# Tile order inside a weight chunk, a bias table written in eight pieces, S5 prefetches tied to late weight loads, and an S5 inner product at foreground priority

## The chip, the cores and the metric

The program runs on one core of a Trainium2 chip. The time is that of one execution in device microseconds (us); three executions of the kernel before were timed, and one further execution was profiled. The engines are named as in the profile: PE is TensorE (its weight loads apart as PEld), DVE is VectorE, ACT is ScalarE, POOL is GpSimd, SP is SyncE, which here only issues DMAs.

## The reference, cut to what matters

Two transformer blocks of width 2048 run over 256 positions in float32.

```python
def first_block(x, p, ...):
    z = rms_norm(x, norm_mix_pre) @ w_in
    y_lru = rglru_mixer(u, g_lru, ...)               # gated recurrence
    y_nsa = nsa_mixer(q, kc, vc, ..., rel_bias)      # sparse attention; bias_tab[rel_bucket(dist)]
    h = x + rms_norm(concat(norms(y_lru, y_nsa)) @ w_out)
    h = h + rms_norm(square(relu(rms_norm(h) @ mlp_w1)) @ mlp_w2)
    return h + sigmoid(h @ ple_gate) * (p @ ple_proj)

def second_block(x, ...):
    # layer 0: stick-breaking attention and gated linear attention, then swiglu_ffn(0)
    # layer 1: s5_mixer, then swiglu_ffn(1)

def s5_mixer(h, ...):        # 128 groups of 16 channels, 64 complex states each
    s_re, s_im = scan(lambda, b @ u)
    y = gelu(c_re @ s_re - c_im @ s_im + d * u)
    val, gate = split(y @ w_glu)
    return val * sigmoid(gate)

def swiglu_ffn(h, w_in, w_out):
    gate, up = split(h @ w_in)
    return (silu(gate) * up) @ w_out
```

## The kernel before, in words

**Dense products.** Activations lie transposed: 128 features on the partitions, T=256 positions in a row. A float32 product is made of fp32r products. A weight chunk lands in a `wr` tile (`wload`, SP issues the DMA at L258); ACT casts it to `wh` (L261), DVE subtracts to get the rest `wl` (L262). X is kept as a high and a low half side by side. For each 128 features of the input (index `kk` in a chunk, usually two to a chunk) and each output tile `j` (usually four, one PSUM bank each) PE does `wh` times both halves (512 columns) and `wl` times the high half (256 columns), both at L304 in `group`. "Narrow" groups put two tiles into a bank and need three matmuls of 256 columns. At a group's end `evac` empties each tile: ACT copies one half (L357), DVE adds the other (L361, or L364 and L365 with a factor), and the bank is free for a later group. PSUM tiles have the tags `ps`, `px` and `pm`.

**Order.** A scheduler orders each engine's instructions by priority, which is the place in the program unless `low(n)` moves it back; each engine runs its list in order. `issue_after(i)` puts an instruction behind `i` in the same engine's list without a wait. A DMA whose completion semaphore is still in use by an earlier DMA waits for that one.

**Background work.** `s5_gen` builds the matrices of the S5 mixer (DRAM tensors `TTd`, `TBd`, `BBd`, `CBd`) while the MLP of the first block and ffn(0) of the second run, at a priority lowered by 100 (`bg_low`). For each of its 16 blocks `prod` does eight small matmuls into one bank `kt` (L1720). In the first mixer a list `self.mix` of generators is advanced by two steps after each chunk (`mix_step`): compression of keys and values, the position bias, and the gated recurrence.

**Bias table.** `bias_tables` makes one row of 511 bias values per head with one matmul (`tb`, 16 partitions), and one DMA of POOL (L608) writes a skewed table `tab` of 16 x 128 x 256 values to DRAM, from which the mixer reads back (`m<-tab`).

**S5 stage.** Eight loads bring `TBd` (L1803) and six bring part of `TTd` (L1901: two into `ttq`, four into an `x` tile); then `carry`, `turn`, `inner` and `outer` run over 8 pairs of feature tiles. `wraw` (L1794) loads `BBd`, `TTd` and `CBd` into slots of the weight pool. After `outer`, ACT applies gelu (L1930), and `relay` (L1812) moves finished ranges of k (`cuts`: 0 to 8, 8 to 12, 12 to 16) from `Yg` to `Yt` in eight SBUF-to-SBUF DMAs each, from 16 partitions apiece. `pre` (L1948, L1949) splits the result into halves for the GLU product, a `group` with `pre`.

Of the kernel before, what the change touches and what calls it, by code (L numbers as in the profile page):

```python
# [57 lines left out]
def layout(inp):  # L58
# [28 lines left out]
    o["relb"] = rb  # L87
    dist = np.arange(511) - 255
    b = np.where(dist >= 0, _rel_bucket(dist), 32)
    oh = np.zeros((33, 2, 511), np.float32)  # L90
    oh[b, 0, np.arange(511)] = 1.0
    oh[:, 1] = oh[:, 0, ::-1]
# [44 lines left out]
class K:  # L137
    def __init__(self, tc, I, out, es, dump=None):
        self.tc, self.nc, self.I, self.out = tc, tc.nc, I, out
        self.es = es  # L140
        self.dumpf = dump
        pool = lambda name, bufs, **k: es.enter_context(tc.tile_pool(name=name, bufs=bufs, **k))
        self.cp = pool("const", 1)
        self.xp = pool("xp", 6)
        self.wp = pool("wp", 4)
        self.ep = pool("ep", 5)
        self.mp = pool("mp", 9)
        self.sp = pool("sp", 4)
# [5 lines left out]
        self.mix, self.mix_n, self.summed = [], 1, None  # L154
        self.hold = ()
# [97 lines left out]
    def wload(self, pieces, shape=(P, 2, 512)):  # L253
# [3 lines left out]
        for sl, src in pieces:  # L257
            nc.sync.dma_start(wr[sl], src)  # L258
# [28 lines left out]
    def group(self, Xk, ks, load, ntile=4, pre=None, narrow=None, tag="ps", kc=2):  # L287
# [17 lines left out]
        for c in range(0, n, kc):  # L305
# [4 lines left out]
            for kk in range(kc):  # L310
                i = c + kk
                X = Xk(ks[i])
                for j in range(ntile):
                    if narrow:
                        mm(ps[j], lhs(wh, kk, j), X[:, 0], i == 0 and j % 2 == 0, False)
                        mm(ps[j], lhs(wh, kk, j), X[:, 1], False, False)
                        mm(ps[j], lhs(wl, kk, j), X[:, 0], False, i == n - 1)
                    else:
                        mm(ps[j], lhs(wh, kk, j), X, i == 0, False)
                        mm(ps[j][:, 0:T], lhs(wl, kk, j), X[:, 0], False, i == n - 1)  # L320
# [274 lines left out]
    def bias_tables(self):  # L595

        nc, I = self.nc, self.I
        relb = self.m([33, 16], tag="relb", bufs=1)
        nc.scalar.dma_start(relb, I["relb"])
        oh = self.wp.tile([33, 2, 511], F32, tag="wr", name="oh")  # L600
        nc.scalar.dma_start(oh, I["oh"])
        ps = self.ps()
        nc.tensor.matmul(ps[0:16, 0:511], relb, oh[:, 1], start=True, stop=True)
        tb = self.m([16, 512])
        nc.vector.tensor_copy(tb[:, 0:511], ps[0:16, 0:511])
# [18 lines left out]
    def block1_in(self):  # L624
# [39 lines left out]
        self.mix, self.mix_n = [self.compress_gen(kk, cmp_), self.bias_gen(), self.lru_gen(L)], 2  # L664
# [854 lines left out]
    def s5_gen(self):  # L1519
# [193 lines left out]
        def prod():  # L1713
# [3 lines left out]
            for i in range(2):  # L1717
                for r in range(4):
                    q = 2 * r + i
                    nc.tensor.matmul(kt[r * 32:r * 32 + 32, 0:P], bt[:, i, r * 32:r * 32 + 32],  # L1720
                                     cx[q // 4][:, q % 4].rearrange("p t h -> p (t h)"), start=(i == 0), stop=(i == 1),
                                     skip_group_check=True)
# [74 lines left out]
    def s5(self):  # L1797
# [126 lines left out]
        def outer(kp):  # L1924
# [83 lines left out]
```

## Time and profile before

| | |
|---|---|
| Median of three executions | 3652.32 us (3651.43 to 3671.67) |
| Profiled execution, its own time | 3657.45 us |
| Its span | 3655.6 us |
| Mean granted TensorE clock | 0.981 |
| PE busy | 3501.3 us, 96% |
| PEld busy | 3060.9 us, 84% |
| DVE, ACT, POOL busy | 64%, 50%, 28% |
| DMA | 699.60 MB, mean 191 GB/s |

PE's busy time is a sum of modelled pipelined intervals, so small gaps between matmuls hide in it. The page's slices show where it falls; the waits show what it stood for. Rows of the trace say start, duration, engine, line, operation, and in brackets the idle time before and what ended it.

### The profile page before, as it was taken

To read this page: it belongs to the slowest core of one execution; us is meant where nothing else is said; L and a number is where in the kernel's file an instruction comes from. 1 tells how busy PE (TensorE), PEld (TensorE's weight loads), DVE (VectorE), ACT (ScalarE), POOL (GpSimd) and SP (SyncE) were. 2 spreads that over 40 slices of the span, in tenths; PEclk is the share of its full clock that TensorE was granted. 3 is DMA by queue.
4 is the path that set the end of the run, shared out by engine and by line. 5 is a ranking of instruction groups with operands and counts; after the bars stand their busy time and mean duration, and the time that the engine had idled before them with its cause. 6 is when DMAs were issued, how large, how long until landed. Compare 5 with 4: busy or idle time off the path is not lost. (4 is left out here: it accounts for less than half of the span.)

```text
span 3655.6 us, 59158 instructions
## 1 busy us (share of the span) xinstructions
PE 3501.3 (96%) x22198; PEld 3060.9 (84%) x22198; DVE 2353.4 (64%) x3610; ACT 1833.1 (50%) x2879; POOL 1022.5 (28%) x1498
## 2 busy tenths in 40 slices
PE   8989999999999999999899999999779999999998
PEld 8888888888888898999787888887668888888887
DVE  6686785567656866546765566566755765555566
ACT  4656654644445654346644444344555544444444
POOL 1231242299620112104334555465400200000000
PEclk9999999999999999999999999999989999999999
DMA  8644456667765564565567776677875466665663
GB/s 216 207 130 151 130 172 189 181 210 211 229 202 187 180 198 135 149 194 187 161 207 227 225 228 211 212 225 246 261 219 185 144 192 188 190 187 188 187 187 127
DMA packets 506551, 699.60 MB, mean 191 GB/s; under 512 B 43239, under 2 KB 317671, under 8 KB 506264
## 3 DMA queue, kind: packets, MB, share of 16 engines
q1 hardware_dynamic: 472848, 628.60, 55.8%
q0 software_dynamic: 27120, 63.05, 5.8%
q10 hardware_dynamic: 6296, 4.17, 0.4%
q8 instruction: 174, 2.85, 0.3%
q14 instruction: 113, 0.93, 0.1%
HBM read 654.22 MB, written 37.22 MB: 189 GB/s over the span
## 5 line engine op out<-in xcount | busy, mean ns | idle before, releaser
L304 PE MATMUL ps<-x,wh 128*128 128x512 f32 (+1 forms) x8560 | 2498.4, 355 | 62.1 <-DVE e L361 19.3
L262 DVE TENSOR_TENSOR wl<-wr,wh 128x1024 fp32r<-128x1024 f32 x1126 | 1441.4, 1285 | 1099.6 <-ACT wh L261 1095.3
L304 PE MATMUL ps<-x,wl 128*128 128x256 f32 x6832 | 1922.4, 283 | 0.8 <-DVE wl L262 0.8
L261 ACT ACTIVATE wh<-wr 128x1024 fp32r<-128x1024 f32 x1126 | 1184.0, 1057 | 1245.0 <-PE ps L304 1051.9
L304 PEld LDWEIGHTS ps<-x,wh 128*128 128x128 f32 x8560 | 1510.7, 191 | 319.5 <-issue 30.3
L304 PEld LDWEIGHTS ps<-x,wl 128*128 128x128 f32 x6832 | 1306.1, 191 | 11.1 <-issue 5.6
L304 PE MATMUL px<-x,wh 128*128 128x512 f32 (+1 forms) x1776 | 658.3, 396 | 11.2 <-DVE x L249 6.8
L304 PE MATMUL px<-x,wl 128*128 128x256 f32 x1744 | 491.7, 282 | 0.5 <-DVE wl L262 0.5
L304 PEld LDWEIGHTS px<-x,wh 128*128 128x128 f32 x1776 | 332.6, 189 | 94.4 <-DVE x L249 8.6
L304 PEld LDWEIGHTS px<-x,wl 128*128 128x128 f32 x1744 | 330.5, 190 | 4.8 <-issue 3.2
L527 POOL TENSOR_TENSOR e<-x,r_c 128x256 f32<-128x256 f32 x40 | 39.8, 1001 | 1051.0 <-DVE r_c L448 1042.8
L357 ACT ACTIVATE e<-ps 128x256 f32<-128x256 f32 x324 | 120.5, 377 | 75.2 <-PE ps L304 63.4
L1762 POOL TENSOR_TENSOR m<-m,m 128x128 f32<-128x128 f32 x128 | 70.3, 573 | 302.5 <-PE pm L1720 302.5
L376 POOL TENSOR_TENSOR acc<-acc,sq 128x256 f32<-128x256 f32 x89 | 78.0, 876 | 252.7 <-ACT sq L375 250.0
L245 ACT ACTIVATE x<-e 128x256 fp32r<-128x256 f32 x168 | 68.2, 411 | 90.1 <-DVE e L1500 47.3
L246 DVE TENSOR_TENSOR x<-e,x 128x256 fp32r<-128x256 f32 x168 | 86.0, 521 | 26.4 <-ACT x L245 22.6
L1761 POOL TENSOR_TENSOR m<-m,m 128x128 f32<-128x128 f32 x128 | 82.7, 671 | 0.7
L1779 POOL TENSOR_TENSOR m<-m,m 128x256 f32<-128x256 f32 x64 | 59.6, 932 | 71.7 <-DMA m<-in_s5bT_dram 71.0
L361 DVE TENSOR_TENSOR e<-ps,e 128x256 f32<-128x256 f32 x168 | 69.9, 416 | 6.4 <-ACT e L357 6.4
L1780 POOL TENSOR_TENSOR m<-m,m 128x256 f32<-128x256 f32 x64 | 73.7, 1152 | 0.1
L738 PE MATMUL ps<-wh,x 128*128 128x512 f32 x160 | 64.6, 404 | 0.0
L740 PE MATMUL ps<-wh,x 128*128 128x512 f32 x160 | 63.2, 395 | 0.0
(488 smaller groups left out, 2895.3 us busy)
## 6 DMA issues: line engine op xcount, KB each, us to landing
wr<-in_w_ffn_in_dram SPq DMA_DIRECT2D x704, 256.0 KB, 3.3
wr<-in_mlp_w_dram SPq DMA_DIRECT2D x256, 512.0 KB, 4.2
wr<-in_w_ffn_out_dram SPq DMA_DIRECT2D x176, 512.0 KB, 4.3
wr<-in_w_in_dram SPq DMA_DIRECT2D x152, 512.0 KB, 3.8
wr<-in_w_out_dram SPq DMA_DIRECT2D x64, 512.0 KB, 4.1
wr<-in_w_glu_dram SPq DMA_DIRECT2D x128, 256.0 KB, 3.1
wr<-in_ple_gate_dram SPq DMA_DIRECT2D x32, 512.0 KB, 4.5
wr<-in_w_in_dram SPq DMA_DIRECT2D x32, 256.0 KB, 4.9
```

Source lines behind the costliest of these rows:

```text
L245: a = nc.scalar.activation(dst[:, 0], src, AF.Copy)
L246: b = (eng or nc.vector).tensor_tensor(dst[:, 1], src, dst[:, 0].bitcast(F32), op=ALU.subtract)
L261: nc.scalar.activation(wh, wr, AF.Copy)
L262: nc.vector.tensor_tensor(wl, wr, wh.bitcast(F32), op=ALU.subtract)
L304: mm = lambda o, w, x, a, z: nc.tensor.matmul(o, w, x, start=a, stop=z, skip_group_check=True)
L357: a = S.activation(t, ps[:, T:2 * T], AF.Copy)
L361: self.hold = a, V.tensor_tensor(y, ps[:, 0:T], t, op=ALU.add)
L376: (eng or nc.vector).tensor_tensor(acc, acc, q, op=ALU.add)
L738: nc.tensor.matmul(ps, xh, wh, start=first, stop=False, skip_group_check=True)
L1761: G_.tensor_tensor(cx[:, q], u_(0), l_(0), op=ALU.mult)
L1762: G_.tensor_tensor(t1[:, q], u_(1), l_(1), op=ALU.mult)
L1780: G_.tensor_tensor(t1, v4(gb[0][:, 1]), v4(gb[1][:, 1 - ri]), op=ALU.mult)
```

## The change

It has five parts.

- **Tile order.** In each chunk `group` now runs all matmuls of tile 0, then of tile 1, and so on. Only in groups with `pre` the chunks before the last keep the old order (all tiles of one `kk`, then of the next).
- **Inner product.** The eight matmuls of `prod` get the priority of foreground work.
- **Bias table.** The table `relb` is repeated eight times, so that `tb` fills 128 partitions; eight POOL DMAs, each from another 16 partitions, write 16 of the 128 rows of `tab` each. They stand in a generator, first in `self.mix`, one per step. `oh` is taken from the `m` pool and not from a `wr` slot.
- **S5 prefetches.** The `TBd` loads are tied behind every third of the last 25 weight loads of ffn(0), and the six `TTd` loads behind the last one.
- **Relays.** From `Yg` to `Yt` the first range is issued by POOL alone, the other two by POOL and SP in turn; ACT issues none.

```diff
@@ bias_tables
-        relb = self.m([33, 16], tag="relb", bufs=1)
+        relb, oh = self.m([33, P], tag="relb", bufs=1), self.m([33, 512])
...
-        oh = self.wp.tile([33, 2, 511], F32, tag="wr", name="oh")
...
-        skew = bass.AP(tensor=tb.tensor, offset=tb.offset + 127, ap=[list(tb.ap[0]), [-1, P], [1, T]])
-        nc.gpsimd.dma_start(self.tab, skew)
+        def gen():
+            for r in range(8):
+                rows = tb[r * 16:r * 16 + 16]
+                nc.gpsimd.dma_start(self.tab[:, r * 16:r * 16 + 16], bass.AP(
+                    tensor=rows.tensor, offset=rows.offset + 127 - 16 * r, ap=[list(rows.ap[0]), [-1, 16], [1, T]]))
+                yield 1
+        self.tab_gen = gen()
...
-        self.mix, self.mix_n = [self.compress_gen(kk, cmp_), self.bias_gen(), self.lru_gen(L)], 2
+        self.mix, self.mix_n = [self.tab_gen, self.compress_gen(kk, cmp_), self.bias_gen(), self.lru_gen(L)], 2
@@ group
-            for kk in range(kc):
+            order = [(kk, j) for j in range(ntile) for kk in range(kc)]
+            if pre and c + kc < n:
+                order = [(kk, j) for kk in range(kc) for j in range(ntile)]
+            for kk, j in order:
@@ s5_gen, prod
-            for i in range(2):
-                for r in range(4):
+            with self.low(-self.bg_low):
+                for i in range(2):
+                    for r in range(4):
@@ s5
+        late = self.loads[-25:]
         for kp in range(8):
-            nc.sync.dma_start(TB[kp // 4][:, kp % 4], self.TBd[kp])
+            with self.tc.issue_after(late[3 * kp].ins):
+                nc.sync.dma_start(TB[kp // 4][:, kp % 4], self.TBd[kp])
...
-                nc.sync.dma_start(tl[:, i], tt_src(len(tts)))
+                with self.tc.issue_after(late[-1].ins):
+                    nc.sync.dma_start(tl[:, i], tt_src(len(tts)))
...
-                    relay(Yg, Yt, k0, k1, (nc.gpsimd, nc.scalar) if i < 2 else (nc.gpsimd, nc.scalar, nc.sync))
+                    relay(Yg, Yt, k0, k1, (nc.gpsimd, nc.sync) if i else (nc.gpsimd,))
```

The first place is PE's list at the end of a group in the MLP of the first block, where the last chunk of one group (`px_7806` to `ps_7809`, and `px_7813` to `ps_7816` after) is followed by the first chunk of the next. Before:

```order
L304 MATMUL px_7806<-x_5333,wh_7966 128x512
L304 MATMUL px_7806<-x_5333,wl_7967 128x256
L304 MATMUL px_7807<-x_5333,wh_7966 128x512
L304 MATMUL px_7807<-x_5333,wl_7967 128x256
L304 MATMUL ps_7808<-x_5333,wh_7966 128x512
L304 MATMUL ps_7808<-x_5333,wl_7967 128x256
L304 MATMUL ps_7809<-x_5333,wh_7966 128x512
L304 MATMUL ps_7809<-x_5333,wl_7967 128x256
L304 MATMUL ps_8056<-x_5332,wh_8062 128x512
```

After, in the same place:

```order
L304 MATMUL ps_7815<-x_5340,wh_7973 128x512
L304 MATMUL ps_7815<-x_5340,wl_7974 128x256
L304 MATMUL ps_7815<-x_5340,wh_7973 128x512
L304 MATMUL ps_7815<-x_5340,wl_7974 128x256
L304 MATMUL ps_7816<-x_5340,wh_7973 128x512
L304 MATMUL ps_7816<-x_5340,wl_7974 128x256
L304 MATMUL ps_7816<-x_5340,wh_7973 128x512
L304 MATMUL ps_7816<-x_5340,wl_7974 128x256
L304 MATMUL ps_8063<-x_5339,wh_8069 128x512
```

The last four pairs of the group went round all four tiles before; now they are the two pairs of the third tile and the two of the fourth, and the first two tiles have ended ahead of them.

The second place is PE's list where the eight matmuls of one block's `prod` (into a `pm` bank) stand among those of ffn(0). Before:

```order
L1720 MATMUL pm_21057<-m_20366,m_20345 32x128
L304 MATMUL px_21094<-x_18759,wh_21209 128x512
L1720 MATMUL pm_21057<-m_20366,m_20345 32x128
L304 MATMUL px_21094<-x_18759,wl_21210 128x256
L1720 MATMUL pm_21057<-m_20596,m_20345 32x128
L304 MATMUL ps_21095<-x_18759,wh_21209 128x512
L1720 MATMUL pm_21057<-m_20596,m_20345 32x128
L304 MATMUL ps_21095<-x_18759,wl_21210 128x256
L304 MATMUL ps_21096<-x_18759,wh_21209 128x512
L1720 MATMUL pm_21057<-m_20366,m_20345 32x128
```

After, for the same block:

```order
L1732 MATMUL pm_21064<-m_20373,m_20352 32x128 x2
L1732 MATMUL pm_21064<-m_20603,m_20352 32x128
L304 MATMUL px_21100<-x_18765,wh_21106 128x512
L1732 MATMUL pm_21064<-m_20603,m_20352 32x128
L304 MATMUL px_21100<-x_18765,wl_21107 128x256
L1732 MATMUL pm_21064<-m_20373,m_20352 32x128
L304 MATMUL px_21100<-x_18765,wh_21106 128x512
L1732 MATMUL pm_21064<-m_20373,m_20352 32x128
L304 MATMUL px_21100<-x_18765,wl_21107 128x256
L1732 MATMUL pm_21064<-m_20603,m_20352 32x128
```

The block before was eight runs of one matmul; after it is a run of three and five of one. Seven of the 16 blocks had eight runs and have six now; eight had five runs (four matmuls and then one at a time), and have five still.

The third place is SP's list where `CBd` is loaded for the last pairs of the S5 stage. Before, the last two loads stand together:

```order
L1794 DMA wl_27905<-CBd 128x1024
L1794 DMA wr_27915<-CBd 128x1024
L1794 DMA wl_27933<-CBd 128x1024
L1794 DMA wr_27943<-CBd 128x1024
L258 DMA wr_27980<-in_w_glu_dram 128x2x256 x2
```

After, four relays of the second range stand between them:

```order
L1806 DMA wl_27912<-CBd 128x1024
L1806 DMA wr_27922<-CBd 128x1024
L1806 DMA wl_27940<-CBd 128x1024
L1826 DMA x_27579<-x_27578 128x1x128 x4
L1806 DMA wr_27950<-CBd 128x1024
L258 DMA wr_27987<-in_w_glu_dram 128x2x256 x2
```

The relays came to SP from ACT's list, and the last load moved behind them.

## Rows read from the trace of the kernel before

**Rows 1.** The page: busy time of the engines, and granted TensorE clock by slices.

```profile
PE 3501.3 (96%) x22198; PEld 3060.9 (84%) x22198; DVE 2353.4 (64%) x3610; ACT 1833.1 (50%) x2879; POOL 1022.5 (28%) x1498
...
PEclk9999999999999999999999999999989999999999
```

**Rows 2.** PE's waits: line waited for, us in total, times, longest us.

```profile
PE ps L304 <- DVE e L361: 19.3, 14, 2.9
PE ps L304 <- ACT wh L261: 14.1, 4, 7.5
...
PE ps L304 <- DVE e L364: 5.5, 5, 3.4
...
PE pm L870 <- ACT wh L261: 2.5, 1, 2.5
```

**Rows 3.** Busy time by stretches; PE first, then the granted clock, DMA share, GB/s.

```profile
100.00:200.00 100.00, 89.07 (x594) 80.64 (x592) 68.96 (x116) 62.18 (x108) 33.93 (x51) 0.92 0.64 192
...
2600.00:2700.00 100.00, 62.77 (x901) 48.57 (x901) 68.35 (x99) 48.85 (x80) 32.73 (x51) 0.78 0.87 261
```

**Rows 4.** PE's timeline at a group end in the MLP of the first block.

```profile
716.54 0.39 PE L304 MATMUL ps<-x,wh 128*128 128x512 f32 x1
...
716.89 0.39 PE L304 MATMUL ps<-x,wh 128*128 128x512 f32 x1
719.13 0.47 PE L304 MATMUL ps<-x,wh 128*128 128x512 f32 x1 [1.85 <-DVE e L361]
```

**Rows 5.** DVE's timeline of the same stretch.

```profile
715.83 1.64 DVE L262 TENSOR_TENSOR wl<-wr,wh 128x1024 fp32r<-128x1024 f32 x1
717.39 1.26 DVE L246 TENSOR_TENSOR x<-e,x 128x256 fp32r<-128x256 f32 x2
718.57 0.41 DVE L361 TENSOR_TENSOR e<-ps,e 128x256 f32<-128x256 f32 x1
```

**Rows 6.** PE's timeline at one block's inner product in ffn(0).

```profile
2118.22 0.43 PE L1720 MATMUL pm<-m,m 128*32 128x128 f32 x8
2118.57 0.50 PE L304 MATMUL ps<-x,wh 128*128 128x512 f32 x1
2119.00 0.41 PE L1720 MATMUL pm<-m,m 128*32 128x128 f32 x2
2119.34 0.39 PE L304 MATMUL ps<-x,wl 128*128 128x256 f32 x1
```

**Rows 7.** Stretch of a block of eight runs, first run to last.

```profile
1992.92:1998.39 5.47, 5.47 (x25) 2.51 (x24) 1.22 (x1) 0.70 (x1) 1.25 (x4) 1.00 0.63 191
```

**Rows 8.** DMA issues, 58 to 92 us: queues; KB each, median us to landing.

```profile
q0 software_dynamic: 528, 2.10, 57.9%
...
tab<-m POOLq DMA_DIRECT2D x1, 2048.0 KB, 25.5
wr<-in_w_in_dram SPq DMA_DIRECT2D x8, 256.0 KB, 14.4
```

**Rows 9.** PE's timeline near 84 us; busy time of 84 to 89 us.

```profile
84.77 0.80 PE L304 MATMUL ps<-x,wh 128*128 128x256 f32 x2 [5.73 <-ACT wh L261]
...
84.00:89.00 5.00, 3.77 (x16) 3.48 (x17) 1.54 (x2) 1.78 (x2) 0.00 (x0) 0.50 1.02 307
```

**Rows 10.** DMA queues and issues from 2604 to 2614 us, relays of the S5 stage.

```profile
q0 software_dynamic: 192, 0.52, 26.3%
...
x<-x POOLq DMA_DIRECT2D x4, 128.0 KB, 5.0
```

**Rows 11.** DMA issues from 2480 to 2520 us, the W2 product of ffn(0).

```profile
wr<-in_w_ffn_out_dram SPq DMA_DIRECT2D x12, 512.0 KB, 5.7
x<-TBd SPq DMA_DIRECT2D x8, 512.0 KB, 7.9
```

**Rows 12.** PE's timeline, stalls at 2010 and 2507 us in ffn(0).

```profile
2010.17 0.50 PE L304 MATMUL ps<-x,wh 128*128 128x512 f32 x1 [1.98 <-DVE x L361]
...
2506.77 0.50 PE L304 MATMUL ps<-x,wh 128*128 128x512 f32 x1 [2.88 <-DVE e L361]
```

**Rows 13.** SP's waits, 2500 to 2700 us; ACT's timeline in the S5 stage.

```profile
SPq L1794 <- DMA x<-x: 12.8, 2, 9.8
...
2673.69 7.88 ACTq L1812 DMA_DIRECT2D x<-x  x4
```

**Rows 14.** PE's timeline at the last outer product of the S5 stage.

```profile
2680.07 1.08 PE L1847 MATMUL px<-wl,x 128*32 128x128 f32 x16 [5.15 <-DMA wl<-CBd]
2683.00 1.08 PE L1847 MATMUL px<-wr,x 128*32 128x128 f32 x16 [1.85 <-DMA wr<-CBd]
```

More of the change, by code (lines that the diff above doesn't have):

```diff
@@ L86, in layout @@
     rb[32] = NEG
-    o["relb"] = rb
+    o["relb"] = np.tile(rb, (1, 8))
     dist = np.arange(511) - 255
     b = np.where(dist >= 0, _rel_bucket(dist), 32)
-    oh = np.zeros((33, 2, 511), np.float32)
-    oh[b, 0, np.arange(511)] = 1.0
-    oh[:, 1] = oh[:, 0, ::-1]
+    oh = np.zeros((33, 512), np.float32)
+    oh[b, 510 - np.arange(511)] = 1.0
     o["oh"] = oh
@@ L154, in __init__ @@
         self.mix, self.mix_n, self.summed = [], 1, None
+        self.loads = []
         self.hold = ()
@@ L257, in wload @@
         for sl, src in pieces:
-            nc.sync.dma_start(wr[sl], src)
+            self.loads.append(nc.sync.dma_start(wr[sl], src))
         wh = self.wp.tile(list(shape), F32R, tag="wh", name=self.nm("wh"))
@@ L309, in group @@
             wh, wl = load(ks[c])
-            for kk in range(kc):
+            order = [(kk, j) for j in range(ntile) for kk in range(kc)]
+            if pre and c + kc < n:
+                order = [(kk, j) for kk in range(kc) for j in range(ntile)]
+            for kk, j in order:
                 i = c + kk
                 X = Xk(ks[i])
[L313 to L320, printed above, removed]
+                if narrow:
+                    mm(ps[j], lhs(wh, kk, j), X[:, 0], i == 0 and j % 2 == 0, False)
+                    mm(ps[j], lhs(wh, kk, j), X[:, 1], False, False)
+                    mm(ps[j], lhs(wl, kk, j), X[:, 0], False, i == n - 1)
+                else:
+                    mm(ps[j], lhs(wh, kk, j), X, i == 0, False)
+                    mm(ps[j][:, 0:T], lhs(wl, kk, j), X[:, 0], False, i == n - 1)
             self.mix_step()
@@ L597, in bias_tables @@
         nc, I = self.nc, self.I
-        relb = self.m([33, 16], tag="relb", bufs=1)
+        relb, oh = self.m([33, P], tag="relb", bufs=1), self.m([33, 512])
         nc.scalar.dma_start(relb, I["relb"])
-        oh = self.wp.tile([33, 2, 511], F32, tag="wr", name="oh")
         nc.scalar.dma_start(oh, I["oh"])
         ps = self.ps()
-        nc.tensor.matmul(ps[0:16, 0:511], relb, oh[:, 1], start=True, stop=True)
-        tb = self.m([16, 512])
-        nc.vector.tensor_copy(tb[:, 0:511], ps[0:16, 0:511])
+        nc.tensor.matmul(ps, relb, oh, start=True, stop=True)
+        tb = self.m([P, 512])
+        nc.vector.tensor_copy(tb, ps)
         self.tab = self.dp.tile([16, P, T], F32, tag="tab", name="tab")
-        skew = bass.AP(tensor=tb.tensor, offset=tb.offset + 127, ap=[list(tb.ap[0]), [-1, P], [1, T]])
-        nc.gpsimd.dma_start(self.tab, skew)
+        def gen():
[5 more added lines that the diff above has]
+        self.tab_gen = gen()
         self.bc = self.c([P, 2, 2, 8, 16], "bc")
@@ L1716, in prod @@
             kt = self.ps()
-            for i in range(2):
-                for r in range(4):
[L1719 to L1722, printed above, removed]
+            with self.low(-self.bg_low):
+                for i in range(2):
+                    for r in range(4):
+                        q = 2 * r + i
+                        nc.tensor.matmul(kt[r * 32:r * 32 + 32, 0:P], bt[:, i, r * 32:r * 32 + 32],
+                                         cx[q // 4][:, q % 4].rearrange("p t h -> p (t h)"), start=(i == 0), stop=(i == 1),
+                                         skip_group_check=True)
             kp = self.m([P, 240])
```

## The prediction

> **What bounds the kernel now.** I read the engines first: PE is busy for 3501.3 us of a span of 3655.6, no other engine for more than 64%, and the granted clock is nearly full throughout [rows 1]. So the work of PE sets the time, and the change removes none of the large products. What it can win is the rest: stalls of PE, the stretches at a lower clock that follow some of them, and small matmuls that break a smooth stream. The waits of PE name the stalls [rows 2]: 19.3 us in 14 waits for an emptied PSUM bank (L361) and 5.5 in 5 for the same with a factor (L364), 14.1 in 4 for a cast weight. The stretches show where little else remains to be won: PE is 100% or nearly so in most of them, but 89% busy at a clock of 0.92 from 100 to 200 us, and 63% at 0.78 from 2600 to 2700, the S5 stage [rows 3]. The profiled execution took 3657.45 us, 5.1 more than the median of 3652.32; each sum below is made against the former and set against the latter at the end. A measurement of this kernel tells a change from none at about 1%, 36.5 us.
>
> **Tile order.** A group of four tiles and two `kk` ends with a chunk of eight pairs of matmuls, 0.35 us apart (716.54 to 716.89) [rows 4]. The last pairs of the four tiles stood at places 5, 6, 7, 8 and now stand at 2, 4, 6, 8. The first tile ends three pairs, 1.05 us, sooner, the second 0.70, the third 0.35, the fourth at the same time. The number of matmuls is the same, and a pair takes 0.35 whichever bank it goes to, so the stream itself costs nothing more. If each of the 19 bank waits became shorter by 1.05 us or vanished, that were 18 us: one end. But the place where PE waits is still the first matmul of the third or fourth tile of the next group, which needs the later banks, and what comes late there is not the end of the tile. At 719.13 PE waits for the L361 that DVE began at 718.57; DVE had been busy with a weight remainder and two splits of X since 715.83, while the tile's last matmul lay well back [rows 4, 5]. A sooner end of that tile moves DVE's list only as far as that list was waiting for it. In ffn(0) the stalls at 2010 and 2507 us [rows 12] stand where weights landed late, and there the order gives nothing. The other end is a loss: in a group with `pre` the last chunk now wants its second X at pair 2 and not at pair 5, 1.05 us sooner; in seven such groups up to 7 us. I take -5, nearer to the rows of 719 than to the 18.
>
> **Inner product.** A run of L1720 costs the same whether long or short: from 2118.22 to 2118.57 four matmuls (eight records), from 2119.00 to 2119.34 one (two records) [rows 6]. A block of eight runs takes 5.47 us [rows 7]; the four pairs of L304 within it are worth 4 x 0.35 = 1.40 [rows 4], so a run costs (5.47 - 1.40) / 8 = 0.51 us with the switch to and fro. The order of instructions shows that the change saves two runs in each of seven blocks and none in the others: 14 x 0.51 = -7. The matmuls were ready one after the other because what feeds them comes in steps and PE takes whatever is ready; a higher priority does not change that. POOL and ACT, which take up the product, have idle time there. There is little to bound on the other side, since the eight come no later: 0.
>
> **Bias table.** The one DMA takes 25.5 us, and in that time the weight loads of SP take 14.4 us in the median [rows 8]. [...] The transfer of `tab` kept engines busy for 0.579 x 16 x 34 = 315 engine-us for 2.10 MB, 150 per MB [rows 8]. Relays from POOL, each from another 16 partitions, took 0.263 x 16 x 10 = 42 for 0.52 MB, 81 per MB [rows 10]. The eight pieces are of that kind; at their rate the table needs 25.5 x 81/150 = 14 us, is done near 75 us, and the weights are there when PE wants them at 79. I take -8. If the pieces gain nothing, 0. If the stall of 2.5 us that follows in the compression (L870) [rows 2] and the low clock behind it go too, since ACT catches up, -14. Against it: the generator takes eight steps of the mixer's list, so compression and recurrence start four chunks later and more of them is left for the end of the list; the nearest row is the 2.5 us of one such wait, so up to +3. `oh` no longer takes a weight slot, which is hidden behind the first loads.
>
> [...]
>
> **S5 prefetches and relays.** The eight loads of `TBd` land in 7.9 us and weights beside them in 5.7 [rows 11]; PE's stall of 2.88 us at 2507 lies in that stretch and the one of 1.98 at 2010 beside the first `ttq` load [rows 12]. Spreading eight loads over 25 weight loads and moving `ttq` behind them can win these 4.9 at best; as POOL's own loads and stores run there too, I take -3. Two more `TTd` loads now stand ahead of `BBd` on SP. At 5.7 to 7.9 us for a landing, and two that overlap, they could delay the stage by up to 5 us if nothing lay between; what lies between is the end of ffn(0) with its norm, which hides them.
>
> In the S5 stage a load of `CBd` waited on SP for 9.8 us until a relay had landed [rows 13], and PE then stood for 5.15 and 1.85 us for the last two [rows 14]. With no relay issued by ACT that wait goes for the first of them, but the second now stands on SP behind four relays, which wait for the gelu of the pair before. The end of the second wait, at 2683.00, thus moves little: between 0 and -7, and I take -2, since a relay and the load behind it are no sooner than before. ACT is free for gelu, having held 7.88 us for its four relays [rows 13]; the last gelu waits for PE, not for that, so it adds -1. The first range now takes eight issues of POOL instead of four; what they feed, the GLU, begins after 2683 [rows 14], and that cover hides them; without it four more issues in a row on POOL, at about the 2 us of a relay's turn in ACT's list (7.88 for four) [rows 13], would cost up to 8.
>
> **Sum.** -5 - 7 - 8 - 3 - 3 = -26 against 3657.45, 3631 for such an execution; against the median, **3626 us**, 0.7% less.
>
> **The rivals.**
> 1. *The bank waits do vanish.* Sooner ends of two tiles let ACT and DVE empty them ahead of the weight work, -18 instead of -5, and the low-clock stretches behind these waits go too (another -8, by three or four stretches at half the 5 us of [rows 9]); with the far end of the table, -14, and of the relays, -8: 3652 - 18 - 8 - 7 - 14 - 8 = 3597. For it: 19 waits of one kind [rows 2]. Against: DVE's full list at 719 [rows 5].
> 2. *X becomes the late one (slower).* The new order wants the second X of a chunk three pairs sooner in the first chunks of groups without `pre` also, where X has just been made. If that makes a wait of 1.05 us in one group of four (some 30 of the 107 wide ones), it costs +31, and it outweighs the gains from about 25 groups on. Time 3652 - 26 + 31 = 3657. Against it: before the change DVE had already made X at most of these places, and the waits for a bank were more than twice as long.
> [...]
> 4. *The inner product does run in one piece.* The change doesn't do what it says by the order of instructions. If it did, one run of 0.51 per block would save 7 x 3.6 + 8 x 2.0 = 41 instead of 7: 3592.
>
> **How the numbers follow.** The forecast has 0.50, rival 1 0.20, rival 2 0.13, rival 3 0.15, rival 4 0.02. The forecast's own range, from its terms' ends, is about 3608 to 3642. Faster by over 1% is a time below 3615.8: rivals 1 and 4, and a tenth to a sixth of the forecast, 0.28. Slower by over 1%, above 3688.8, needs rival 2 at twice its size: 0.03. The range leaves out half of rivals 1 and 2: 3597 to 3658.
>
> **What would show it.** In the trace after: no stall near 79 us and the eight pieces landed by about 75; runs of L1732 in sixes and fives; the total of waits for L361 and L364 near 20 us, still at third and fourth tiles; the last `CBd` load issued behind four relays, PE's wait for the load before it gone. The prediction is wrong if PE's bank waits fall under 10 us (rival 1), or waits for X grow by over 15 (rival 2).

## The result and the profile after

The changed kernel takes 3609.18 us in the median against 3654.62 for the kernel before beside it: a ratio of 0.9864, 95% interval 0.9831 to 0.9896. That is 50 us less (38 to 62) by the ratio, where 26 were forecast (the two medians differ by 45); the time lies in the range, near its fast end. The profiled execution has a span of 3607.2 us against 3655.6.

The page of the changed kernel, engines and granted clock by slices, answers to [rows 1]:

```profile
PE 3480.9 (96%) x22198; PEld 3050.9 (85%) x22198; DVE 2342.4 (65%) x3610; ACT 1833.5 (51%) x2879; POOL 1026.8 (28%) x1510
...
PEclk9999999999999999999999999999889999999999
```

PE still bounds the kernel and runs as many instructions as before; its busy time fell by 20 us and the time without work by 28. PE's waits in the changed kernel (line waited for, us in total, times, longest us), where L365 and L368 are the old L361 and L364:

```profile
PE ps L304 <- DVE x L249: 15.7, 11, 3.7
...
PE ps L304 <- DVE e L365: 9.7, 8, 4.1
PE ps L304 <- ACT wh L261: 8.7, 2, 7.7
...
PE px L1861 <- DMA wr<-CBd: 6.8, 1, 6.8
...
PE ps L304 <- DVE e L368: 1.9, 2, 1.4
```

The waits for an emptied bank fell from 19.3 + 5.5 us [rows 2] to 9.7 + 1.9, those for a cast weight from 14.1 to 8.7. A third row of bank waits, where L361 writes X at once, fell from 6.3 us in 5 waits to 2.5 in 2. The waits for X did not grow out of measure (13.7 us in 8 waits in the full list of before, 15.7 in 11 now). One wait in the S5 stage is new: 6.8 us for a load of `CBd`.

Busy time by stretches in the changed kernel answers to [rows 3] (PE first; then the granted clock, the share of the DMA engines, GB/s):

```profile
100.00:200.00 100.00, 93.03 (x646) 84.19 (x645) 67.58 (x111) 61.07 (x100) 35.34 (x57) 0.97 0.61 187
...
2600.00:2700.00 100.00, 79.77 (x677) 66.60 (x678) 62.75 (x81) 53.05 (x80) 14.29 (x24) 0.88 0.70 214
```

From 100 to 200 us PE is busy 93% at 0.97 in place of 89% at 0.92. The second row can't be set against its like without care: the S5 stage begins some 45 us sooner, and half of it has moved into the stretch ahead.

Where the time went is read by stages. The main product has 19008 records of PE at L304 in every trace, so the start of the k-th in one trace can be set against the k-th of another. The stages are: the first mixer (records 0 to 1200, to 252 us in the kernel before), the rest of the first block with the mixer of the second (to 9600, 1807 us), ffn(0) (to 13200, 2496 us), its end and the S5 stage (to 13700, 2700 us), the rest. Differences to the trace of before, in us, up to the last large product, one profiled execution each; the last columns are the timed ratios and their intervals:

```
run                   mixer   block1    ffn0  end+S5   rest    sum   ratio   95% interval
changed kernel         -9.4     -7.8   -20.6    -8.4   -1.9  -48.2   0.9864  0.9831-0.9896
a_alone                 1.1     -0.5     0.2    -2.9   -2.8   -4.9   0.9971  0.9956-0.9987
b_alone                -0.2     -1.9   -19.5    -6.2    2.9  -24.9   0.9904  0.9885-0.9923
c_alone                -8.8     -3.5     3.9     0.8    0.3   -7.3   1.0000  0.9986-1.0014
de_alone               -3.9      5.2     1.1    -2.7    3.2    2.8   0.9991  0.9980-1.0002
kt_copy_late            0.5      9.2    -0.9    -7.2    1.3    2.8   1.0015  1.0003-1.0027
kt_copy_late_tied      -1.9      5.4   -18.1    -0.5    0.1  -14.9   0.9950  0.9932-0.9968
pool_light_before       0.7     -7.4   -11.2    -1.6   -0.6  -20.1   0.9960  0.9944-0.9976
pool_light_b            0.7    -14.2    29.7    -8.3   -1.3    6.7   1.0016  1.0006-1.0025
all_but_bias_table     -4.2     -3.0   -20.0    -8.8    1.8  -34.4   0.9896  0.9878-0.9913
all_but_tile_order    -10.5     -2.8   -20.0   -13.0    1.8  -44.6   0.9883  0.9864-0.9902
all_but_tied_loads     -9.2     -9.5   -18.1    -8.4   -0.6  -45.8   0.9884  0.9868-0.9900
cb_first               -8.6    -11.5   -19.7  -10.7     1.1  -49.4   0.9870  0.9855-0.9885
```

A stage of one trace is not exact: de_alone has nothing in the first two stages and differs there by -3.9 and 5.2 (its mixer ran at a granted clock of 0.96 in place of 0.94), so a difference of up to about 5 us is not read by itself.

Two columns speak at once. Every run with the pieces of the bias table has 8.6 to 10.5 us less in the mixer, and there PE is without work for 19 us (after, c_alone) against 29 to 31 (before, de_alone, all_but_bias_table). Every run with the new priority of the inner product and all the background's work has 18 to 21 us less in ffn(0), whatever else it holds. Three of the seven blocks that lose two runs lie in ffn(0), so the sum of the prediction had 3 of its 7 us there.

### The profile page after: what moved, and what is told of

It reads as the page before. It is cut to its first block, busy times and chain, and to the rows that moved or that the text cites. A ratio compares the mean times of both kernels' runs of the same rounds, so it can differ in the third digit from the quotient of the medians.

```text
span 3607.2 us, 59167 instructions
## 1 busy us (share of the span) xinstructions
PE 3480.9 (96%) x22198; PEld 3050.9 (85%) x22198; DVE 2342.4 (65%) x3610; ACT 1833.5 (51%) x2879; POOL 1026.8 (28%) x1510
## 4 chain that ended last, share of the span: by engine, by line
PE 85%; DVE 7%; ACT 3%; issue 2%; DMA 1%; POOL 1%; SPq 0%; ACTq 0%; DVEq 0%; POOLq 0%
PE ps L304 62%; PE px L304 16%; DVE wl L262 2%; DVE x L532 1%; PE ps L749 1%; ACT wh L261 1%; PE ps L750 1%; PE ps L751 1%; DVE e L531 1%; PE pm L1732 1%; DVE x L249 1%; DMA wr<-in_w_in_dram 1%; PE px L971 0%; PE px L1361 0%; PE pm L1017 0%
## 5 line engine op out<-in xcount | busy, mean ns | idle before, releaser
L304 PE MATMUL ps<-x,wh 128*128 128x512 f32 (+1 forms) x8560 | 2471.5, 354 | 41.6 <-DVE x L249 15.7
L304 PE MATMUL ps<-x,wl 128*128 128x256 f32 x6832 | 1920.8, 282 | 0.5 <-DVE wl L262 0.4
L304 PEld LDWEIGHTS ps<-x,wh 128*128 128x128 f32 x8560 | 1508.6, 191 | 291.7 <-issue 24.9
L304 PEld LDWEIGHTS ps<-x,wl 128*128 128x128 f32 x6832 | 1303.6, 191 | 7.9 <-issue 2.4
L304 PE MATMUL px<-x,wh 128*128 128x512 f32 (+1 forms) x1776 | 639.2, 395 | 11.3 <-DVE x L249 6.9
L304 PE MATMUL px<-x,wl 128*128 128x256 f32 x1744 | 491.5, 282 | 0.8 <-DVE wl L262 0.8
L304 PEld LDWEIGHTS px<-x,wh 128*128 128x128 f32 x1776 | 332.3, 188 | 94.3 <-DVE x L249 9.1
L304 PEld LDWEIGHTS px<-x,wl 128*128 128x128 f32 x1744 | 330.1, 189 | 6.1 <-issue 3.8
L361 ACT ACTIVATE e<-ps 128x256 f32<-128x256 f32 x324 | 120.2, 372 | 69.9 <-PE ps L304 58.4
L246 DVE TENSOR_TENSOR x<-e,x 128x256 fp32r<-128x256 f32 x168 | 77.9, 472 | 24.2 <-ACT x L245 20.2
L1791 POOL TENSOR_TENSOR m<-m,m 128x256 f32<-128x256 f32 x64 | 61.9, 967 | 67.2 <-DMA m<-in_s5bT_dram 66.5
L365 DVE TENSOR_TENSOR e<-ps,e 128x256 f32<-128x256 f32 x168 | 69.8, 417 | 3.8 <-ACT e L361 3.8
L1793 POOL TENSOR_TENSOR m<-m,m 128x256 f32<-128x256 f32 x64 | 69.3, 1082 | 0.7
L1792 POOL TENSOR_TENSOR m<-m,m 128x256 f32<-128x256 f32 x64 | 65.8, 1028 | 0.2
L749 PE MATMUL ps<-wh,x 128*128 128x512 f32 x160 | 64.5, 403 | 1.0 <-ACT wh L261 1.0
```

The source lines that it names most:

```text
L246: b = (eng or nc.vector).tensor_tensor(dst[:, 1], src, dst[:, 0].bitcast(F32), op=ALU.subtract)
L304: mm = lambda o, w, x, a, z: nc.tensor.matmul(o, w, x, start=a, stop=z, skip_group_check=True)
L361: a = S.activation(t, ps[:, T:2 * T], AF.Copy)
L365: self.hold = a, V.tensor_tensor(y, ps[:, 0:T], t, op=ALU.add)
L749: nc.tensor.matmul(ps, xh, wh, start=first, stop=False, skip_group_check=True)
L1793: G_.tensor_tensor(ob[:, :, ri], ob[:, :, ri], t1, op=(ALU.subtract, ALU.add)[ri])
```

## The experiments

**Each part alone.** Four kernels each take one part of the diff into the kernel before, with nothing else.

```diff
# a_alone: group
-            for kk in range(kc):
+            order = [(kk, j) for j in range(ntile) for kk in range(kc)]
# b_alone: prod
+            with self.low(-self.bg_low):
# c_alone: bias_tables and the mixer's list
+        self.mix, self.mix_n = [self.tab_gen, self.compress_gen(kk, cmp_), self.bias_gen(), self.lru_gen(L)], 2
# de_alone: s5
+            with self.tc.issue_after(late[3 * kp].ins):
...
+                    relay(Yg, Yt, k0, k1, (nc.gpsimd, nc.sync) if i else (nc.gpsimd,))
```

Tile order alone, as expected of it:

> Only the tile order inside a chunk is changed in the kernel before. The prediction's theory: about 5 us less, with PE's waits for L361 and L364 still above 18 us. Rival 1 (sooner tile ends let the banks be emptied in time): 15 to 25 us less, most of it between the start of ffn(0) and its end, and those waits below 12 us. Third theory, from the changed kernel's trace: the group-end stalls of ffn(0) came from DVE work that takes 3 us in place of 1.2 while POOL is busy (L262 at 2250.69 took 3.56 us), and the tile order does not move POOL's work, so only a few us less.

Measured: 11 us less by the ratio (5 to 16). Its bank waits stayed. PE's waits of this run, first row of the list, where L363 is the old L361:

```profile
PE ps L304 <- DVE e L363: 21.3, 13, 4.3
```

Nothing changed in ffn(0) (0.2 us), so rival 1 falls: the sooner end of the first tiles did not empty the banks in time. Where the 11 us lie, the trace (4.9 us less, no stage with more than 2.9) does not say.

The inner product alone:

> Only the priority of the inner product is changed in the kernel before. The prediction's theory: 7 us less, 1 us in each of seven blocks. Third theory: POOL's work follows the inner product, so its bursts fall elsewhere against the group ends, and ffn(0) becomes 10 to 20 us shorter, with slow L262 no longer at a group end. If the runs alone count, ffn(0) is at most 5 us shorter.

Measured: 35 us less (28 to 42), the largest part by far, 19.5 of its trace's 24.9 in ffn(0), where the third theory had 10 to 20. The runs on PE are as forecast. PE's timeline in the changed kernel at one block of six runs:

```profile
1959.28 0.42 PE L1732 MATMUL pm<-m,m 128*32 128x128 f32 x6
1959.63 0.50 PE L304 MATMUL px<-x,wh 128*128 128x512 f32 x1
...
1963.24 0.38 PE L304 MATMUL px<-x,wl 128*128 128x256 f32 x1
```

From 1959.28 to 1963.24 are 3.96 us with 0.94 of L304 in them (three of 0.235 and two of 0.117), 3.02 for six runs or 0.50 each, against 8 x 0.51 [rows 7]. The runs explain 7 us and no more; 28 of the 35, or 18 of the trace's 25, were still to be found.

The bias table alone:

> Only the bias table is changed in the kernel before. The prediction's theory: 8 us less, all of it between 60 and 110 us, no stall near 79 us; the table is written in about 14 us. [...] The rest of the kernel should not move by more than 2 us.

Measured: the same time (ratio 1.0000, that is 5 us either way), with 8.8 us less in the mixer and 3.9 more in ffn(0) in its trace. The stage answers for the mechanism, the whole does not resolve it.

Prefetches and relays alone:

> Only the S5 prefetches and the relay issuers are changed in the kernel before. The prediction's theory: 6 us less, 3 of it in ffn(0) (the stalls at 2010 and 2507 us), 3 in the S5 stage. Rival: nothing in the S5 stage, since the last load of CBd stands behind four relays (one wait of about 7 us in place of two of 5.2 and 1.9).

Measured: 3 us less (7 less to 1 more). In the S5 stage 2.7 less, with one wait of 5.6 us for `CBd`. In ffn(0) nothing: the two stalls that the tied loads were to take away are still there. PE's timeline of de_alone, against [rows 12]:

```profile
2011.86 0.50 PE L305 MATMUL ps<-x,wh 128*128 128x512 f32 x1 [2.02 <-DVE x L362]
...
2508.75 0.50 PE L305 MATMUL ps<-x,wh 128*128 128x512 f32 x1 [2.53 <-DVE e L362]
```

The four ratios together are 0.0134 below one, the whole change 0.0136: the parts add up, within their intervals.

**What the earlier product brings beside shorter runs.** The rows of the kernel before show two things that the earlier product could end. ACT's waits from 1800 to 2600 us:

```profile
ACT m L1725 <- PE pm L1720: 33.0, 11, 4.9
```

ACT takes its list in order; standing up to 4.9 us for the product, it might hold up the casts behind (the ACT theory). The new priority brings the product 80 matmuls (14 us) earlier, and of this wait 10.2 us in 4 are left in b_alone. POOL stands for the product too, from 1800 to 2600 us in the kernel before:

```profile
POOL m L1762 <- PE pm L1720: 259.1, 11, 86.8
```

So an earlier product pulls all of POOL's work behind it forward: its products for the B matrices (L1779 to L1781) begin 78 to 85 matmuls sooner in b_alone. Where they fall can matter (the phase theory). This is DVE's timeline of the kernel before at a group's end, ahead of the stall at 2256.75:

```profile
2247.81 1.23 DVE L262 TENSOR_TENSOR wl<-wr,wh 128x1024 fp32r<-128x1024 f32 x1 [1.60 <-ACT wh L261]
...
2250.69 3.56 DVE L262 TENSOR_TENSOR wl<-wr,wh 128x1024 fp32r<-128x1024 f32 x1 [0.43 <-ACT wh L261]
```

The same instruction takes 1.23 us and then 3.56. POOL's timeline beside it:

```profile
2251.03 0.75 POOL L1781 TENSOR_TENSOR m<-m,m 128x256 f32<-128x256 f32 x1
2251.73 0.75 POOL L1779 TENSOR_TENSOR m<-m,m 128x256 f32<-128x256 f32 x1
2252.42 0.73 POOL L1780 TENSOR_TENSOR m<-m,m 128x256 f32<-128x256 f32 x1
```

Five of the stalls between 2000 and 2550 us (2010, 2257, 2309, 2507, 2550) stand behind DVE work that was 2.2 to 4.3 us longer in the 8 us before than its usual, for stalls of 1.9 to 3.4. Three more of ffn(0) (1912, 2158, 2406; 5.9 us together) stand behind weights that landed late. ACT's cast ahead of the last of them:

```profile
2401.34 1.06 ACT L261 ACTIVATE wh<-wr 128x1024 fp32r<-128x1024 f32 x1 [2.28 <-DMA wr<-in_w_ffn_in_dram]
```

With the earlier product the slow remainders are still there, but elsewhere. DVE's timeline of b_alone:

```profile
2222.78 5.29 DVE L262 TENSOR_TENSOR wl<-wr,wh 128x1024 fp32r<-128x1024 f32 x2 [0.73 <-ACT wh L261]
```

Two remainders in 5.29 us, no stall of PE follows.

Three kernels were made to tell the two theories apart. In the first ACT's copy of the product is emitted where it is first used; PE's list is that of before.

```diff
         def prod():
-            S.activation(kp[:, 112:240], kt[:, 0:P], AF.Copy)
-            return kp
+            return kp, kt
         def toep(kp):
+            kp, kt = kp
+            S.activation(kp[:, 112:240], kt[:, 0:P], AF.Copy)
```

> The kernel before, with ACT's copy of the finished inner product (L1725) emitted where its result is first used, some ten places later in ACT's list; PE's list is the same as before. ACT theory (with the product late, ACT stands up to 4.9 us for it, 47.7 us in 14 waits, and the casts and copies behind it come late): those waits vanish and the time falls by 15 us or more, without any of the 7 us that fewer runs on PE give. Phase theory (POOL's bursts slow DVE at group ends, and the earlier product moves them elsewhere): the waits vanish, the time stays within 5 us, and slow L262 remain ahead of the stalls at 2010, 2256 and 2507 us.

Measured: 5 us more (1 to 10), ACT's waits for the product gone, and the stall at 2010 gone with them; where those of 2257 and 2507 were, 0.7 and 1.1 us are left. Both expectations missed, for a reason that neither had. Its trace has one new stall on PE:

```profile
1977.95 0.80 PE L304 MATMUL ps<-x,wh 128*128 128x512 f32 x1 [14.18 <-DVE e L361]
```

ACT at the same place, and SP's waits from 1800 to 2600 us in the same run:

```profile
1974.46 1.06 ACT L261 ACTIVATE wh<-wr 128x1024 fp32r<-128x1024 f32 x1 [16.30 <-DMA wr<-in_w_ffn_out_dram]
```

```profile
SPq L1902 <- DMA TTd<-m: 27.8, 2, 19.4
```

The copy is later, so the store of `TTd` is; a `ttq` load on SP waits 19.4 us for that store, and the weight loads behind it wait too. Without this one stall its ffn(0) would be some 15 us shorter than before, not 0.9.

The second and third kernels leave out the background's products for the B matrices.

```diff
-                for ri in range(2):
-                    G_.tensor_tensor(ob[:, :, ri], v4(gb[0][:, 0]), v4(gb[1][:, ri]), op=ALU.mult)
-                    G_.tensor_tensor(t1, v4(gb[0][:, 1]), v4(gb[1][:, 1 - ri]), op=ALU.mult)
-                    G_.tensor_tensor(ob[:, :, ri], ob[:, :, ri], t1, op=(ALU.subtract, ALU.add)[ri])
+                G_.memset(ob, 0.0)
```

In the kernel before:

> The kernel before, with the six products and sums of the background that make the B matrices (L1779 to L1781, 64 of each pair) left out and a fill of the tile in their place, so the S5 mixer's values are not computed; all DMAs stay. Phase theory: POOL no longer slows DVE in these bursts, L262 over 3 us vanish in ffn(0), and the time falls by 10 to 20 us, as stalls of 2 to 3.5 us at 2010, 2256, 2309, 2507 and 2550 go. ACT theory: the time stays within 5 us, since the product comes as late as before.

Measured: 15 us less (9 to 20), 11.2 in ffn(0), although ACT's wait is as long as before. ACT's waits of this run, from 1800 to 2600 us:

```profile
ACT wh L261 <- DMA wr<-in_w_ffn_in_dram: 50.0, 21, 8.1
ACT wh L261 <- DMA wr<-in_w_ffn_out_dram: 33.8, 16, 7.6
ACT m L1725 <- PE pm L1720: 33.0, 11, 4.9
```

So POOL's products have a price of their own, as the phase theory has it: the stalls at 2010, 2257, 2309 and 2507 are gone. (The background's transfers move too, and two stalls of 1.7 and 2.0 us are new.) The theory's other sign failed: remainders over 3 us did not vanish, 13 of 14 are counted in ffn(0). Eleven of them stand in both runs beside other products of POOL, those for the C matrices (L1761 to L1763) right behind the inner product, and take 4.5 to 6.1 us there without a stall of PE; the three beside L1779 to L1781 are gone, and two of 3.1 us are new. And with the new priority:

> The kernel before with the inner product's new priority and with the same background products left out as in the run beside it (the S5 values are not computed). Phase theory: in this order the bursts already miss the group ends, so little is left to win: 3630 to 3620, that is 30 to 40 us below the kernel before, and the difference to the run beside it shrinks to 10 to 20 us. ACT theory: the full 28 to 35 us of the priority stand between the two runs.

Measured: 6 us more than the kernel before, where both theories had 10 to 40 less. The time is lost in ffn(0) (29.7 us). PE and then ACT at the first such stall:

```profile
1874.82 0.80 PE L304 MATMUL ps<-x,wh 128*128 128x512 f32 x1 [5.36 <-DVE e L364]
```

```profile
1871.96 1.06 ACT L261 ACTIVATE wh<-wr 128x1024 fp32r<-128x1024 f32 x1 [5.86 <-DMA wr<-in_w_ffn_in_dram]
```

Weights land late here, and PE has 12 stalls of 0.8 to 5.9 us. But they land as late in the run beside it. ACT's waits for weights here, from 1800 to 2600 us:

```profile
ACT wh L261 <- DMA wr<-in_w_ffn_in_dram: 64.9, 17, 7.5
...
ACT wh L261 <- DMA wr<-in_w_ffn_out_dram: 20.2, 8, 4.2
```

That is 85.1 us against 83.8 there (50.0 + 33.8). There PE is without work for 7.7 us of ffn(0), here for 35.3. The long waits come some 80 matmuls sooner here, as the product does (one of 5.5 us at the 10275th large product of the trace, where the other run has 8.1 at the 10359th), and fall on the ends of groups. So it is again the place that costs, of late weights this time. Why weights land late in both was not tried, and of ACT's wait the run tells nothing.

**The late copy with the prefetches tied.** The wait of SP in kt_copy_late is what the tie of the `ttq` loads takes away. So the late copy was run with the tie (relays as before):

```diff
+        late = self.loads[-25:]
...
+            with self.tc.issue_after(late[3 * kp].ins):
...
+                with self.tc.issue_after(late[-1].ins):
```

> The kernel before with ACT's copy of the product emitted later (as in the run kt_copy_late; PE's list is that of before) and with the S5 prefetches tied behind the late weight loads of ffn(0). If a late copy without the tie lost its gain in one wait of SP (ttq behind the store of TTd, 14 us of PE at 1978), that wait is gone here and the time falls by 12 to 18 us below the kernel before; most stalls of ffn(0) stay away. If the late copy itself is worth nothing, the time stays within 4 us of before.

Measured: 18 us less (12 to 25), and 18.1 in ffn(0), as much as with the new priority, with the order on PE untouched. PE's waits, L362 being the old L361:

```profile
PE ps L305 <- DVE e L362: 10.5, 10, 2.9
```

Against 19.3 [rows 2]. So in ffn(0) the extra gain is not one of PE's order at all. Nor is it one of ACT's wait. ACT's timeline around the wait ahead of the stall at 2257, in the kernel before:

```profile
2238.44 1.06 ACT L261 ACTIVATE wh<-wr 128x1024 fp32r<-128x1024 f32 x1 [1.76 <-PE ps L304]
2241.75 0.28 ACT L1725 ACTIVATE m<-pm 128x128 f32<-128x128 f32 x1 [2.25 <-PE pm L1720]
2243.90 1.06 ACT L261 ACTIVATE wh<-wr 128x1024 fp32r<-128x1024 f32 x1 [1.87 <-PE ps L304]
```

and at the same matmuls with the late copy and the tie:

```profile
2233.44 1.06 ACT L262 ACTIVATE wh<-wr 128x1024 fp32r<-128x1024 f32 x1 [1.81 <-PE ps L305]
2238.89 1.06 ACT L262 ACTIVATE wh<-wr 128x1024 fp32r<-128x1024 f32 x1 [4.39 <-PE ps L305]
```

The second cast begins 5.46 us after the first with the wait for the product and 5.45 without it, for ACT then stands for PE. Behind all 14 products that ACT stands for in the kernel before, the next cast begins at the same matmul of PE's list in both. The wait held up no cast, and the ACT theory falls.

What the late copy does move is POOL's work behind it and the background's transfers. The remainder that took 3.56 us at 2250.69 begins at the same place here, 1.33 us after the same matmul. DVE, then POOL:

```profile
2245.68 1.35 DVE L263 TENSOR_TENSOR wl<-wr,wh 128x1024 fp32r<-128x1024 f32 x1
```

```profile
2245.92 1.72 POOL L1783 TENSOR_TENSOR m<-m,m 128x256 f32<-128x256 f32 x1
```

POOL's products for the B matrices still fall on this group's end, but now one of them takes 1.72 us in place of 0.75, and DVE's remainder 1.35 in place of 3.56. The three stalls behind late weights are gone as well. Busy time of ffn(0) as above, in the kernel before, in b_alone and in this run:

```profile
1807.01:2496.36 689.35, 675.14 (x3779) 564.41 (x3777) 415.76 (x473) 303.23 (x428) 340.89 (x500) 0.99 0.71 219
```

```profile
1804.90:2474.80 669.90, 666.16 (x3778) 560.12 (x3777) 421.80 (x473) 302.09 (x428) 350.17 (x513) 1.00 0.73 225
```

```profile
1810.60:2481.90 671.30, 669.35 (x3779) 561.00 (x3778) 406.61 (x473) 302.19 (x427) 351.35 (x498) 1.00 0.72 224
```

PE is without work for 14.2, 3.7 and 2.0 us. Behind three of the stalls of before (2010, 2257, 2406) the granted clock was 0.50 for 3.4 us each, in b_alone once, in the last run never; a pair of matmuls took 0.64 us there (2257.55 to 2258.19 in the kernel before) against the 0.35 of [rows 4], which makes 1.5 us lost of each 3.4 by estimate, or 4.5, 1.5 and 0 in all. With the 3 us of shorter runs, b_alone's 19.5 us have 10.5 + 3.0 + 3 = 16.5, the late copy's 18.1 have 12.2 + 4.5 = 16.7. So the gain in ffn(0) is stalls that are gone, and the low clock behind them.

**Each part undone.** Three kernels are the changed one without one part.

Without the bias table's pieces:

> The changed kernel with the bias table as before (one DMA, not in the mixer's list). The prediction's theory: 8 us more than the changed kernel, about 3617 to 3620, with the stall near 79 us back. If what the table wins at 60 to 110 us is lost again behind, as the run of the table alone says (no change in the whole), 3609, the same as the changed kernel.

Measured: 0.9896 against 0.9864, 12 us more, with intervals that overlap; the mixer has 4.2 us less than before in place of 9.4 (de_alone, without the pieces too, 3.9 less). The stall is back. PE's waits from 60 to 120 us in this run:

```profile
PE ps L305 <- ACT wh L262: 5.8, 1, 5.8
PE pm L873 <- ACT wh L262: 2.5, 1, 2.5
```

Both are absent from the changed kernel. Its DMA queues and issues from 58 to 92 us:

```profile
q0 software_dynamic: 640, 2.10, 31.9%
...
wr<-in_w_in_dram SPq DMA_DIRECT2D x14, 256.0 KB, 6.0
tab<-m POOLq DMA_DIRECT2D x8, 256.0 KB, 10.1
```

The same 2.10 MB kept engines busy for 0.319 x 16 x 34 = 174 engine-us, against 315 [rows 8]; the eight pieces, issued from 59.63 us on, had all landed at 78.63, after 19.0 us.

Without the tile order:

> The changed kernel with the tile order as before. The prediction's term: 5 us more than the changed kernel (ratio to before about 0.988). By the run of the tile order alone (0.9971): 10 us more (0.989). Rival 1 (the order empties banks in time): 15 us or more, with waits for L361 and L364 above 20 us in all.

Measured: 0.9883, 7 us more than the changed kernel, with overlapping intervals; its waits for L361 are 12.5 us against 9.7. The prediction's 5 and the 10 of the part alone both fit; rival 1's 15 with waits above 20 does not.

Without the tied loads:

> The changed kernel with the loads of TBd and TTd where they were, the relays as changed. The prediction's term: 3 us more than the changed kernel. If the tie protects the earlier product from waits of SP for TTd, more than 8 us more, and SP's wait for TTd in ffn(0) above 5 us. If it does nothing once the product is early, the same within 4 us.

Measured: 0.9884, 7 us more, with overlapping intervals, and a wait of SP for `TTd` of 4.8 us. This lies between the forecasts of 3 and of more than 8. ffn(0) has 18.1 us less than before in place of 20.6, and b_alone, also without the tie, 19.5: what the tie is worth in that stage once the product is early is not resolved.

**A load ahead of the relays.** The new wait of 6.8 us comes from SP's list. PE's timeline in the changed kernel answers to [rows 14], and SP's to [rows 13]:

```profile
2636.66 1.08 PE L1861 MATMUL px<-wr,x 128*32 128x128 f32 x16 [6.76 <-DMA wr<-CBd]
```

```profile
2627.45 3.81 SPq L1826 DMA_DIRECT2D x<-x  x4
2631.35 1.20 SPq L1806 DMA_DIRECT2D wr<-CBd  x1
```

The last load is issued behind the four relays. The experiment fetches each pair's `CBd` one pair earlier:

```diff
+            for k in (kp * 2 + 8, kp * 2 + 9):
+                if 8 <= k < 16:
+                    cbs.append(self.wraw(self.CBd[k], ("wl", "wr")[k % 2]))
             pt = turned(ps, True).rearrange("p (j g c) -> p g j c", j=2, g=8)
```

> The changed kernel with the last loads of CBd issued one pair earlier on SP, ahead of the four relays of the second range. If the wait of 6.76 us at 2636.66 is the order on SP, it falls below 1.5 us, and the S5 stage and the whole become 4 to 6 us shorter than the changed kernel. If the load is late for the transfers beside it, it lands no sooner than the relays and the gain is under 2 us.

Measured: 0.9870, the same as the changed kernel. The wait is gone and another took its place. PE's timeline, then ACT's:

```profile
2628.18 0.62 PE L1861 MATMUL px<-wr,x 128*32 128x128 f32 x16
...
2636.16 1.22 PE L304 MATMUL px<-x,wh 128*128 128x512 f32 x2 [5.83 <-ACT wh L261]
```

```profile
2635.05 1.06 ACT L261 ACTIVATE wh<-wr 128x1024 fp32r<-128x1024 f32 x1 [1.73 <-DMA wr<-in_w_glu_dram]
```

The GLU's first weights still come behind the four relays, and PE waits 5.83 us for their cast instead of 6.76 for `CBd`. In the trace the stage is 2 us shorter (-10.7 against -8.4); in the time that is not seen. No version was found that beats the changed kernel beyond its interval.

## Why the prediction was right, and where its sum was short

The time lies in the range, but not by its sum: 50 us against 26, and most of the rest is one effect that the sum had at 0. It stands at the fast end of the forecast's own range (3608), which was made of far ends of other terms, so that it lies inside is in part luck.

- **Tile order, -5.** Right in that the bank waits stay: 21.3 us in 13 alone, against 19.3 in 14, and 11 of the 14 stalls of over 0.9 us behind a bank stand at the same matmul as before, within one. Measured 11 (5 to 16) alone and about 7 undone, so the size held too. That it comes from shorter bank waits, as the term has it, is not shown: the wait at 719 is 2.79 us long with the new order alone, against 1.85. Whether the waits are still at third and fourth tiles the trace can't say, as it does not tell the banks apart. The loss that was feared for groups with `pre` doesn't show.
- **Inner product, -7.** The term itself holds: two runs fewer in each of seven blocks, 0.50 us a run against 0.51. But the part is worth 35, and the step that failed is "POOL and ACT, which take up the product, have idle time there. There is little to bound on the other side, since the eight come no later: 0". They come 14 us sooner, and POOL's idle time was POOL standing for the product (259.1 us in 11 waits from 1800 to 2600), so its work and its transfers come sooner with them. What this moves was put at 0 and is worth 28 us by the ratio, 18 by the trace; in ffn(0) it is 10.5 us of PE without work and 3.0 of low clock.
- **Why that costs PE.** Leaving out POOL's products for the B matrices gives 11 us in ffn(0), with the product as late and ACT's wait as long as before. The late copy with the tie gives 18 (the tie by itself, in de_alone, nothing there) and moves neither a matmul nor a cast ahead of a group's end, only POOL's work and the background's transfers. So the stalls come from where the background falls: on DVE's work at a group's end (2010, 2257, 2507, 2550), or on weight loads (1912, 2158, 2406). ACT's wait, 33.0 us in 11, was not the cause. What decides whether DVE's instruction or POOL's takes longer, and why weights land late at these places, was not varied and stays open. Some 10 us of the 35 are not in b_alone's trace at all (the ratio goes by several executions, the trace by one); they are not placed.
- **Bias table, -8.** No run shows the 8 as one figure. The kernel before shows the stall of 5.73 us and 5 us at a granted clock of 0.50 behind it [rows 9]; in these, three matmuls of 256 columns took 0.64 us (86.41 to 87.05) against 0.36 at a clock of 1.00 (89.70 to 90.06), by estimate up to 2.2 us lost. Right in place: the stall near 79 us is gone, and PE is without work for 10 us less in the mixer. The stage is 8.6 to 10.5 us shorter in all five traces that hold the pieces; against the 4 us that two runs without them show too, the share of the table lies between 5 and 10. The stall of 2.5 us in the compression (L870), which the prediction let go only at its far end of -14, is gone as well; a wait of 2.3 (L889) has come. The transfer was mis-sized: 19.0 us, not 14. Its engine time was right, 174/2.10 = 83 engine-us per MB against the 81 of the relays, but the time did not shrink with it. The 6.5 us less were enough for the first weight behind the table to be cast from 79.59 on, and PE did not run dry. In the whole the part alone is not resolved (0, 5 either way), undone it is about 12. A stall that stays, the 0.15 of rival 3, did not come.
- **Prefetches and relays, -6.** Measured 3 (7 less to 1 more). The -3 for the prefetches rests on a misreading: no weight landed late ahead of the stalls at 2010 and 2507, DVE's work took longer there, and tying the loads left both in place (2.02 and 2.53 us). In the S5 stage the wait for the load behind four relays was foreseen: 5.15 went, 1.85 became 6.76 (5.6 with this part alone), 2.7 us less in the trace.
- **The signs.** Waits for L361 and L364 were to stay near 20 us and came to 11.6, just above the 10 that stood for rival 1. It is not rival 1: with the tile order alone they are 26.0, with the inner product alone 13.2. Waits for X grew by 2 us; rival 2 falls. Rival 4's condition, one run per block, is not met; its 3592 was nearly reached by another way.

## What to carry to other kernels

An instruction that is moved has two prices: what it costs on its own engine, and what its consumers do sooner or later with it. Ask of every moved result which in-order engine stands for it, and where the work behind then falls; here by the ratio four fifths of that part's gain lay there. A wait of a consumer is not yet a price: ACT stood 33.0 us for the product and no cast was later for it, so look whether the next thing on the path begins later. Work in the background should be looked at for where its bursts and transfers fall against the moments at which the foreground has no slack: POOL's products for the B matrices stood before stalls of 1.9 to 3.4 us at group ends, and beside those for the C matrices DVE's remainders took up to 6.1 us in the stream, with no stall behind them.

## What the runs showed that was not expected

- The same DVE subtraction of 128x1024 took 1.22 us with no product of POOL beside it (2244.99), 1.23 beside one that took 1.57 (2247.81 and 2248.07), and 3.56 beside a row of POOL products of which those quoted took 0.73 to 0.75 us each: 2.3 us more, longer than one of them. At the same place in another run one of POOL's took 1.72 us and the subtraction 1.35.
- A transfer of 2.10 MB from sixteen partitions took 25.5 us, and eight of an eighth each, from sixteen other partitions each, 19.0 us together, with about half the engine time (174 engine-us against 315).
- One DMA that waits for a store, in a list of weight loads, cost PE 14.18 us at once.
